# Turning one more quarter of the mixed activation with a transposing DMA in a two-layer encoder

## The chip, the cores and the metric

The kernel runs on one core of a Trainium2 chip. The metric is the device time of one execution in microseconds (us), as the median of several runs. The core has five engines with a queue of instructions each: TensorE (PE, matrix products and transposes), VectorE (DVE), ScalarE (ACT), GpSimd (POOL) and SyncE (SP), which here issues the DMA transfers. Each queue runs in order; engines wait for one another through semaphores. PEld is the weight load of TensorE, which overlaps its matmuls.

## The reference

The program is a trunk of two layers (DEPTH = 2) over 256 tokens of width 1024, all in float32. In each layer a normed input is projected; a branch A (gated linear attention) and a branch B (grouped-query attention) are formed; they are gated and mixed, and the mix goes through an output projection with a norm and a residual add:

```python
branch_a = (o_gla * jax.nn.silu(gg)) @ w_o_gla
branch_b = gqa_attention(q, k, v) @ w_o_attn
mixed = jax.nn.sigmoid(gate_a) * branch_a + jax.nn.sigmoid(gate_b) * branch_b
h = h + rms_norm(mixed @ w_out, g_mix_post)
gate, up = jnp.split(rms_norm(h, g_ffn_pre) @ w_ffn_in, 2, axis=-1)
h = h + rms_norm((jax.nn.silu(gate) * up) @ w_ffn_out, g_ffn_post)
```

A small embedding per layer follows. The case is about `mixed`, between the line that forms it and `mixed @ w_out`.

## The kernel before

**Tiling.** The 256 tokens are two halves of 128 (`hf` 0 and 1), each filling the partitions. Activations lie with tokens on the partitions; to be the stationary operand of a projection they must be turned, so that features lie on the partitions. Every float32 operand of a matmul is split into a high part (a cast on ScalarE, L112) and a low part (a subtraction on VectorE, L108), and a product is three matmuls: high by high, high by low, low by high (`mm3`, issued at L96). A `Split` object holds the turned and split activation: eight blocks of 128 features, in two groups of four.

**Weights** stream from HBM in units of 1 MB or less through two raw buffers (tag `raw`). ScalarE and VectorE split each unit in two pieces into `wh` and `wl`. When a projection is done with a unit, `ws.done()` starts the splitting of a further one, and with it the next load (L260 on SP, which waits until VectorE has freed the raw buffer).

**Two ways to turn.** `transpose_in` (L429) does four PE transposes of 128x128 into one PSUM bank (`aux`, L433), and then splits from PSUM with raised priority (`put`). `turn_words` (L391) goes without TensorE: a copy on ScalarE separates the two 16-bit halves of each word (L401), a DMA with transpose issued on SP turns them (L407), a second copy on ScalarE joins the halves again (L420), and then the same split follows, from SBUF. It takes three tiles of the pool `t512`, which has seven.

**Order.** Turning is a `Task`, a generator that is run up to its first `yield` when it is created; the number yielded says after how many ticks it goes on. A tick falls in `amode` after every six matmuls of 512 columns, or after twelve of 256. `turn_words` yields SENT = 3 between its first copy and the DMA, and LANDED = 9 between the DMA and the second copy; the PE way yields WAIT_MIX = 3. `Split.need` runs a task to its end where its result is about to be read. So ticks set where an instruction stands in the program. A compile-time scheduler then orders each engine's queue by priority and by what it holds ready, and can put an instruction well ahead of its place in the program (or, inside `high_priority(AHEAD)`, with a head start of 400); `issue_after` pins an order.

**Around the change.** The merge (L1203 to L1219) goes over two column halves `j` of 512, and in each over the two branches; each projection uses all four (`hf`, weight half) combinations. Branch A's product is multiplied by its gate into `sgate[0]`, branch B's into `sgate[1]`, and the two are added (L1212); the tile shows as `big_0gate` or `big_1gate`. That quarter of the mix, 128 tokens by 512 columns, is then handed to a turning task for the `Split` named `mixT` (shown as `big_0merge`, `big_1merge`). The output projection follows (`by_half`, L659, shown as `acc_0wout`): first the whole of `hf` 0, which reads group 0 of `mixT` and then group 1, as 48 matmuls of 512 columns; then `hf` 1, whose columns are cut into 512, 256 and 256, again with group 0 and then group 1. After each half, `after_out` does the norm with residual add and the norm ahead of the FFN: square sums on ScalarE (L471), the inverse root on GpSimd (L483, L487), products and adds on VectorE (L105, L531, L491), and then PE transposes of the normed half.

Of the kernel before, what the change touches and what calls it, by code (L numbers as in the profile page):

```python
# [50 lines left out]
def trunk_kernel(ctx: ExitStack, tc: tile.TileContext, a: dict, out: bass.AP):  # L51
# [52 lines left out]
    def vmul(out, in0, in1):  # L104
        nc.vector.tensor_tensor(out=out, in0=in0, in1=in1, op=ALU.mult)  # L105
# [323 lines left out]
    def transpose_in(sp, src, k, n, hf, plain=None):  # L429

        ps = aux()
        for i in range(n):
            nc.tensor.transpose(ps[:, i * P : (i + 1) * P], src[:, i * P : (i + 1) * P], ident)  # L433
        with tc.high_priority(AHEAD):
            sp.put(ps[:, : n * P], k, n, hf * P, P)
        if plain is not None:
            nc.scalar.copy(plain, ps[:, : n * P])
# [211 lines left out]
    def project(sp):  # L649

        o = [acc(), acc()]
        for kh in range(2):
            w = ws.take()
            for hf in range(2):
                amode(o[hf], sp, hf, kh * 4, w, kh == 0, kh == 1)
            ws.done()
        return o
# [146 lines left out]
    for l in range(DEPTH):  # L804
# [399 lines left out]
        mixT = Split()  # L1204
        ogate.need()
        for j in range(2):
            for br, src in enumerate((gT, aT)):
                for hf, o in enumerate(project(src)):
                    sl = [s[:, hf, j * 512 : (j + 1) * 512] for s in sgate]
                    vmul(sl[br], o, sl[br])  # L1210
                    if br == 1:
                        nc.vector.tensor_tensor(out=sl[0], in0=sl[0], in1=sl[1], op=ALU.add)  # L1212

                        def turn(src=sl[0], hf=hf):
                            yield WAIT_MIX
                            transpose_in(mixT, src, 4, 4, hf)

                        turn = turn() if j else mixT.turn_words(sl[0], 0, 4, hf)
                        mixT.makers[hf].append(Task(turn, part[0], j))  # L1219

        if l + 1 < DEPTH:
# [232 lines left out]
```

## Time and profile before

| | |
|---|---|
| median of 3 runs | 924.8 us |
| lowest and highest | 924.55 and 925.81 us |
| the profiled execution | 924.19 us |
| span in its profile | 922.5 us |
| clock of TensorE granted, mean | 0.997 |

The span runs from the first to the last instruction that the profiler recorded. In the rows shown below, a row of the timeline gives start, duration, engine, line, operation, what it writes and reads, how many instructions were merged into the row, and in brackets the idle time before it and what ended it. A row of the chain gives start, duration, engine, tile and line. Tile names carry the layer and the stage: `wl_0merge` is a low weight part of layer 0 allocated in the merge.

### The profile page before, as it was taken

How to read it: one execution, taken by the hardware profiler on the slowest of the kernel's cores; microseconds unless marked ns; L12 is line 12 of the kernel's file. 1: busy time of each engine (PE TensorE's matmuls, PEld its weight loads, DVE VectorE, ACT ScalarE, POOL GpSimd, SP SyncE). 2: the span in 40 equal slices, each digit the busy share in tenths (PEclk: the TensorE clock that was granted, in tenths of full speed). 3: DMA queues.
4: the chain of work that ended last, by engine and by line, in shares of the span. 5: the costliest groups of instructions: out<-in, count | busy, mean ns of one | idle time of the engine just before them, and what ended most of it. 6: DMA issues, size and time to landing. Idle time of an engine off the chain costs nothing.

```text
span 922.5 us, 12213 instructions
## 1 busy us (share of the span) xinstructions
PE 909.2 (99%) x4577; PEld 771.5 (84%) x4577; DVE 724.3 (79%) x921; ACT 626.1 (68%) x1002; POOL 82.6 (9%) x150
## 2 busy tenths in 40 slices
PE   8999999999999999999999999999999999999996
PEld 7999888888878888887889988888888788888885
DVE  4798977546579998998689789665666799989874
ACT  4668678746468787676765786776455788857663
POOL 3400211100000000000123002100001000000000
PEclk9999999999999999999999999999999999999998
DMA  7564456967377675847555524497564867666551
GB/s 233 171 213 152 137 167 161 291 201 227 95 239 239 174 249 199 267 146 241 176 183 183 183 92 143 143 241 250 194 199 136 276 206 221 217 248 174 184 181 47
DMA packets 119897, 177.12 MB, mean 192 GB/s; under 512 B 35159, under 2 KB 58199, under 8 KB 119838
## 3 DMA queue, kind: packets, MB, share of 16 engines
q1 hardware_dynamic: 119838, 176.34, 59.9%
q8 instruction: 36, 0.59, 0.3%
q14 instruction: 23, 0.19, 0.1%
HBM read 167.41 MB, written 1.05 MB: 183 GB/s over the span
## 4 chain that ended last, share of the span: by engine, by line
PE 75%; DVE 10%; DMA 6%; ACT 4%; issue 3%; POOL 2%; SPq 0%; POOLq 0%; ACTq 0%; DVEq 0%
PE acc_1ffnin L96 10%; PE acc_0ffnin L96 6%; PE acc_1gate L96 5%; PE acc_0gate L96 5%; PE acc_1merge L96 5%; PE acc_0merge L96 5%; PE acc_1ffnin L574 4%; DVE wl_0ffnin L108 3%; PE acc_1gqk L96 2%; PE acc_0rq L96 2%; PE acc_0gqk L96 2%; DMA raw_0ffnin<-in_w_ffn_out_dram 2%; PE acc_1ple L96 2%; PE acc_1gg L96 2%; PE acc_0gg L96 2%
## 5 line engine op out<-in xcount | busy, mean ns | idle before, releaser
L96 PE MATMUL acc_0ffnin<-wh_0ffnin,big_0ffnin 128*128 128x512 f32 x176 | 56.3, 392 | 0.0
L96 PE MATMUL acc_1ffnin<-wh_1ffnin,big_1ffnin 128*128 128x512 f32 x176 | 56.2, 391 | 0.0
L108 DVE TENSOR_TENSOR wl_1ffnin<-raw_1ffnin,wh_1ffnin 128x1024 fp32r<-128x1024 f32 x38 | 45.0, 1218 | 6.4 <-ACT wh_1ffnin L112 6.4
L112 ACT CAST wh_0ffnin<-raw_0ffnin 128x1024 fp32r<-128x1024 f32 x38 | 38.3, 1050 | 17.1 <-DMA raw_0ffnin<-in_w_ffn_out_dram 14.6
L112 ACT CAST wh_1ffnin<-raw_1ffnin 128x1024 fp32r<-128x1024 f32 x38 | 38.4, 1048 | 17.0 <-DMA raw_1ffnin<-in_w_ffn_out_dram 8.9
L108 DVE TENSOR_TENSOR wl_0ffnin<-raw_0ffnin,wh_0ffnin 128x1024 fp32r<-128x1024 f32 x38 | 44.9, 1219 | 6.1 <-ACT wh_0ffnin L112 6.1
L96 PEld LDWEIGHTS acc_1ffnin<-wh_1ffnin,big_1ffnin 128*128 128x128 f32 x176 | 33.0, 188 | 7.1 <-DVE big_1ffnin L108 0.2
L96 PEld LDWEIGHTS acc_0ffnin<-wh_0ffnin,big_0ffnin 128*128 128x128 f32 x176 | 33.0, 188 | 7.1 <-DVE big_0ffnin L108 0.2
L112 ACT CAST wh_0ffnin<-lent_0ffnin 128x1024 fp32r<-128x1024 f32 x30 | 30.2, 1050 | 10.2 <-DVE lent_0ffnin L289 4.0
L108 DVE TENSOR_TENSOR wl_0ffnin<-lent_0ffnin,wh_0ffnin 128x1024 fp32r<-128x1024 f32 x30 | 35.3, 1218 | 1.6 <-ACT wh_0ffnin L112 1.6
L112 ACT CAST wh_1ffnin<-lent_1ffnin 128x1024 fp32r<-128x1024 f32 x30 | 30.2, 1050 | 8.9 <-PE acc_1ffnin L96 3.5
L108 DVE TENSOR_TENSOR wl_1ffnin<-lent_1ffnin,wh_1ffnin 128x1024 fp32r<-128x1024 f32 x30 | 35.3, 1217 | 1.2 <-ACT wh_1ffnin L112 1.2
L96 PE MATMUL acc_0ffnin<-wl_0ffnin,big_0ffnin 128*128 128x512 f32 x88 | 34.4, 391 | 0.1
L96 PE MATMUL acc_1ffnin<-wl_1ffnin,big_1ffnin 128*128 128x512 f32 x88 | 34.4, 391 | 0.1
L574 PE MATMUL acc_1ffnin<-wh_1ffnin,mid_1ffnin 128*128 128x512 f32 x96 | 31.0, 390 | 0.0
L574 PE MATMUL acc_0ffnin<-wh_0ffnin,mid_0ffnin 128*128 128x512 f32 x96 | 31.0, 390 | 0.0
L96 PE MATMUL acc_1ffnin<-wh_1ffnin,big_1wout 128*128 128x512 f32 x96 | 30.4, 389 | 0.0
L96 PE MATMUL acc_0ffnin<-wh_0ffnin,big_0wout 128*128 128x512 f32 x96 | 30.3, 389 | 0.0
L108 DVE TENSOR_TENSOR wl_1gate<-raw_1gate,wh_1gate 128x1024 fp32r<-128x1024 f32 x14 | 16.5, 1221 | 15.2 <-ACT wh_1gate L112 15.2
L108 DVE TENSOR_TENSOR wl_0gate<-raw_0gate,wh_0gate 128x1024 fp32r<-128x1024 f32 x14 | 16.7, 1235 | 12.3 <-ACT wh_0gate L112 12.3
L96 PE MATMUL acc_0rq<-wh_start,big_start 128*128 128x384 f32 (+1 forms) x96 | 25.4, 349 | 0.9 <-ACT big_start L123 0.9
L96 PE MATMUL acc_1gate<-wh_1gate,big_0ple 128*128 128x512 f32 x80 | 24.8, 389 | 0.0
(659 smaller groups left out, 2964.4 us busy)
## 6 DMA issues: line engine op xcount, KB each, us to landing
raw_0ffnin<-in_w_ffn_out_dram SPq DMA_DIRECT2D x11, 1024.0 KB, 5.7
raw_1ffnin<-in_w_ffn_out_dram SPq DMA_DIRECT2D x11, 1024.0 KB, 5.0
lent_0ffnin<-in_w_ffn_in_dram SPq DMA_DIRECT2D x6, 1024.0 KB, 7.6
lent_1ffnin<-in_w_ffn_in_dram SPq DMA_DIRECT2D x6, 1024.0 KB, 5.3
raw_0rq<-in_w_in_dram SPq DMA_DIRECT2D x4, 1024.0 KB
raw_0v<-in_w_in_dram SPq DMA_DIRECT2D x4, 1024.0 KB
raw_0gg<-in_w_in_dram SPq DMA_DIRECT2D x4, 1024.0 KB, 5.1
raw_0gate<-in_w_o_gla_dram SPq DMA_DIRECT2D x4, 1024.0 KB, 5.9
```

What stands on the lines that cost most here:

```text
L96: return nc.tensor.matmul(o, lhsT, rhs, start=start, stop=stop)
L108: nc.vector.tensor_tensor(out=out, in0=in0, in1=in1, op=ALU.subtract)
L112: cast = nc.scalar.copy(hi, src)
L574: nc.tensor.matmul(o, x, y, start=first and k + n == 0, stop=k == 3 and n == 2, skip_group_check=not first)
```

## The change

The task for the second column half (`j` = 1) of the second token half (`hf` = 1) is made with `turn_words` instead of `transpose_in`. The second column half of the first token half keeps its PE transposes, and the first column half keeps `turn_words` for both token halves. Beside the way of turning, this changes the task's waits from WAIT_MIX (3 ticks, then everything) to SENT and LANDED (3 ticks to the DMA, 9 more to the copy back and the split). It is done in both layers.

```diff
@@ -1215,7 +1215,7 @@
                             yield WAIT_MIX
                             transpose_in(mixT, src, 4, 4, hf)
 
-                        turn = turn() if j else mixT.turn_words(sl[0], 0, 4, hf)
+                        turn = turn() if j and hf == 0 else mixT.turn_words(sl[0], 4 * j, 4, hf)
                         mixT.makers[hf].append(Task(turn, part[0], j))
 
         if l + 1 < DEPTH:
```

The core of `turn_words`, which the edited line now calls for this quarter too (here `hf` is given and `far` is false):

```python
def turn_words(self, src, k, n, hf=None, far=False):
...
    x = lambda: t512()[:, : n * P * (2 if hf is None else 1)]
    w = x()
    w16 = w.bitcast(U16)
    nc.scalar.copy(
        w16.rearrange("p (s c) -> p s c", s=2), src.bitcast(U16).rearrange("p (c s) -> p s c", s=2)
    )
    yield SENT
    r, z = [t[:, : n * P * (2 if hf is None else 1)] for t in halves(mid())] if far else (x(), None)
    r16 = r.bitcast(U16)
    nc.sync.dma_start_transpose(out=r16.rearrange("p (r t) -> p r t", t=P), in_=w16)
    yield LANDED
    z = x() if z is None else z
    z16 = z.bitcast(U16)
...
        else:
            nc.scalar.copy(z16.rearrange("p (c s) -> p s c", s=2), r16.rearrange("p (s c) -> p s c", s=2))
            self.put(z, k, n, hf * P, P)
```

## The prediction

> **What bounds the kernel now.** I read the page first: busy time and the chain that ended last. Then I read the chain in order of time around the two places where the edited task runs.
>
> ```profile
> span 922.5 us, 12213 instructions
> PE 909.2 (99%) x4577; PEld 771.5 (84%) x4577; DVE 724.3 (79%) x921; ACT 626.1 (68%) x1002; POOL 82.6 (9%) x150
> PE 75%; DVE 10%; DMA 6%; ACT 4%; issue 3%; POOL 2%; SPq 0%; POOLq 0%; ACTq 0%; DVEq 0%
> ```
>
> TensorE is busy 99% of the span and holds 75% of the chain, so what is taken off TensorE's own queue counts, unless another engine's answer is then late. ScalarE (68%) has room on average; whether it has room here is a question for its queue. The chain at the end of the merge, in layer 0 and then layer 1:
>
> ```profile
> 190.16 43.52 PE acc_0merge L96 x192
> 233.67 4.09 PE acc_0wout L96 x18
> 238.63 6.84 PE acc_0wout L96 x30
> 253.32 1.15 DVE wl_0wout L108
> 254.90 6.11 DMA raw_0wout<-in_w_ffn_in_dram
> ...
> 642.74 43.52 PE acc_1merge L96 x192
> 686.26 4.09 PE acc_1wout L96 x18
> 691.22 6.84 PE acc_1wout L96 x30
> 705.90 1.14 DVE wl_1wout L108
> 707.48 5.00 DMA raw_1wout<-in_w_ffn_in_dram
> ```
>
> The chain is TensorE through the merge and the first token half of the output projection. It breaks once between the 18th and the 19th matmul of that projection (237.76 to 238.63 in layer 0): there the eight PE transposes stand, after three ticks of six matmuls. After that it goes over VectorE's splitting of weights and a load of FFN weights. The two layers run alike, 452.6 us apart.
>
> **The change part by part.** The edit touches one task per layer: the turning of the second 512 columns for tokens 128 to 255. Removed are four PE transposes (one `transpose_in`). TensorE around them:
>
> ```profile
> 237.37 0.40 PE L96 MATMUL acc_0wout<-wh_0merge,big_0merge 128*128 128x512 f32 x1
> 237.60 1.03 PE L433 MATMUL aux_0merge<-ident,big_0gate 128*128 128x128 f32 x8
> 238.39 0.47 PE L96 MATMUL acc_0wout<-wh_0merge,big_0merge 128*128 128x512 f32 x1
> 238.70 0.39 PE L96 MATMUL acc_0wout<-wl_0merge,big_0merge 128*128 128x512 f32 x1
> ```
>
> The eight occupy the queue from 237.60 to 238.39, 0.79 us or 0.10 us each, since they are pipelined. Around them matmuls start 0.23 us apart (237.37 to 237.60), and one step after them is 0.31 us; I leave that bubble in place, because four transposes remain. So four transposes give 4 x 0.10 = **0.40 us** a layer, 0.79 us in two. All of it is on the chain. Bounds: nothing if what follows is late anyway, 0.87 us a layer if the whole gap were the second group's; I take 0.40.
>
> One rule of the Trainium skill would price this higher. "TensorE: Matmul & The Clock Gate", Part 4: PE-mode transpose, gives about 275 ns for one 128x128 transpose in a kernel, and eight at that price are an estimated 2.2 us. The trace agrees with such a duration (272 ns, row below) but not with such a step.
>
> The removed cast and subtraction out of PSUM come back from SBUF at nearly the same length. Added per layer are a copy into 16-bit planes (L401), a transposing DMA (L407) and a copy back (L420). The same three stand in the trace for the first 512 columns:
>
> ```profile
> 211.31 1.05 ACT L401 COPY t_0merge<-big_0gate 128x1024 uint16<-128x1024 uint16 x1 [2.80 <-DVE big_0gate L1212]
> 214.16 1.04 ACT L401 COPY t_0merge<-big_0gate 128x1024 uint16<-128x1024 uint16 x1
> 212.38 4.08 SPq L407 DMA_TRANSPOSE t_0merge<-t_0merge  x2
> 216.45 1.37 ACT L420 COPY t_0merge<-t_0merge 128x1024 uint16<-128x1024 uint16 x1 [1.25 <-DMA t_0merge<-t_0merge]
> 220.09 1.36 ACT L420 COPY t_0merge<-t_0merge 128x1024 uint16<-128x1024 uint16 x1
> 221.64 1.28 DVE L108 TENSOR_TENSOR big_0merge<-t_0merge,big_0merge 128x512 fp32r<-128x512 f32 x2
> L407 SPq DMA_TRANSPOSE t_0merge<-t_0merge x2: 1235/1244/1253, 212.4 to 215.2; - x2
> DMA to landing us min/median/max: 2.4/4.0/8.0
> ```
>
> That is 1.04 + 1.37 = 2.4 us more on ScalarE and 1.24 us more on SP's queue per layer. The first transfer lands 4.07 us after its issue (212.38 to 216.45); all transposing DMAs of the kernel lie between 2.4 and 8.0. From first copy to last subtraction the second half's path was 214.16 to 222.92, 8.8 us, with every wait in it. Now where these fall in the new place:
>
> ```profile
> 233.71 2.00 ACT L112 CAST wh_0merge<-raw_0merge 128x1024 fp32r<-128x1024 f32 x2 [3.43 <-PE acc_0merge L96]
> 238.23 1.07 ACT L112 CAST big_0merge<-aux_0merge 128x512 fp32r<-128x512 f32 x2 [2.52 <-PE aux_0merge L433]
> 242.84 0.60 ACT L471 ACTIVATE t_0wout<-acc_0wout 128x512 f32<-128x512 f32 x1 [3.53 <-PE acc_0wout L96]
> 245.56 0.60 ACT L471 ACTIVATE t_0wout<-acc_0wout 128x512 f32<-128x512 f32 x1 [2.03 <-PE acc_0wout L96]
> 234.44 0.69 DVE L1212 TENSOR_TENSOR big_0gate<-big_0gate,big_0gate 128x512 f32<-128x512 f32 x1
> 235.05 2.35 DVE L108 TENSOR_TENSOR wl_0merge<-raw_0merge,wh_0merge 128x1024 fp32r<-128x1024 f32 x2
> 231.75 6.60 SPq L260 DMA_DIRECT2D raw_0merge<-in_w_ffn_in_dram  x4
> 254.48 3.19 SPq L260 DMA_DIRECT2D raw_0wout<-in_w_ffn_in_dram  x4
> 251.12 0.40 PE L96 MATMUL acc_0wout<-wl_0merge,big_0merge 128*128 128x512 f32 x1
> ```
>
> The sum that is turned is ready at 235.13. ScalarE finishes its two weight casts at 235.71 and idles 2.52 us, so the first copy runs 235.71 to 236.75, covered by that idle time. If the cover were gone it would push the cast at 238.23, which TensorE needs for matmul 25 near 239.46. On SP the last two of the four loads wait until VectorE frees their buffer at 237.40, so the transposing DMA can go out at 236.75 and take 1.24 us; the loads behind it go 0.6 us later, and their weights are cast only from 248.75 on, so this costs nothing. No other issue follows before 254.48. Behind the loads instead, it would go out at 238.35.
>
> Landing: 236.75 + 4.07 = 240.8. The copy back ends near 242.2, the cast near 242.8, the subtraction near 243.5. ScalarE idles 3.53 us ahead of 242.84, VectorE is free until 243.56, so this is covered too. TensorE first reads the result just before 251.12 (one matmul after 250.9; 250.5 with 0.40 us saved): 7 us of slack by this sum, and 6 us by the older path's 8.8 us from 235.71.
>
> The wait added is the copy back's for the landing. Queued behind it on ScalarE, by time, are the two square sums at 242.84 and 245.56. Through GpSimd and VectorE they set when the normed first half is ready for its transposes:
>
> ```profile
> 251.90 1.42 DVE L491 SCALAR_TENSOR_TENSOR mid_0wout<-h,rstd_0wout,mid_0wout 128x512 f32<-128x512 f32 x2 [0.86 <-POOL rstd_0wout L487]
> 253.24 3.49 DVE L108 TENSOR_TENSOR wl_0wout<-raw_0merge,wh_0wout 128x1024 fp32r<-128x1024 f32 x3
> 253.65 1.03 PE L433 MATMUL aux_0wout<-ident,mid_0wout 128*128 128x128 f32 x8
> 248.75 1.03 ACT L112 CAST wh_0wout<-raw_0merge 128x1024 fp32r<-128x1024 f32 x1
> ```
>
> The normed half is complete at 253.32 and TensorE reaches it at 253.65, 0.33 us of slack. The whole row of square sum, scale, norm, weight split and next load hangs on the end of the first half's matmuls, and so moves 0.40 us earlier with them. That is why I let the gain reach the end. Nothing there is bound by a clock of its own: at most two raw buffers are under way, and each load starts on a release.
>
> **Sum:** 2 x 0.40 = 0.79 us of the profiled execution's 924.19 us (span 922.5 us), giving 923.4; that execution is 0.6 us under the median of 924.8, from which I get 924.8 - 0.8 = **924.0 us**. A measurement of this kernel can tell about 0.2%, 1.85 us, from no change, so this is a forecast of no visible change, with a slight lean down.
>
> **The rivals.**
>
> First, *slower: ScalarE's queue is held ahead of the first half's cast.* The compile-time scheduler orders ScalarE; if it puts the copy back in front of the cast at 238.23, the cast waits for landing and copy: 240.82 + 1.36 + 0.59 = 242.8, where TensorE wants it at 239.46. That is 3.3 us lost and 0.4 won, 2.9 a layer, 5.8 in all: **930.6 us**. For it: the copy back ran 11 us ahead of its twelve ticks in the first columns (12 x 6 x 0.23 = 16 us after the creation near 211.5, against 216.45), and ScalarE idled 1.25 us for the landing, so that order is not kept by ticks. Against it: the first half's cast has raised priority and its input is there at 238.2, 1.4 us after the transposing DMA's issue, below the 2.4 us minimum of the landings. It decides where the landing assumed by the scheduler is under 1.4 us. Chance 0.10.
>
> Second, *slower: the landing is late and holds the square sums.* If the transfer goes behind the loads or needs the 8.0 us maximum, it lands at 244.75; copy (1.36) and cast (0.54) end at 246.65, the first square sum with its read takes 0.68, the second starts at 247.33 instead of 245.16. Of these 2.2 us the slack takes 0.33, so 1.84 is lost and 0.4 won: +1.44 a layer, **927.7 us** at most. It decides from a landing near 242.9. For it: four weight loads surround the place. Against it: under the same loads the first columns took 4.07 us. Chance 0.14.
>
> The Trainium skill speaks against the change here: "VectorE: DVE Perf Modes", The three transpose paths, has 390 ns on TensorE against 1309 ns by DMA for 128x128 bf16, and its Rules for kernel authors take TensorE where PSUM will do. Exposed, four such differences would cost an estimated 3.7 us a layer; the trace shows the longer path too (8.8 us against 237.60 to 240.14), but under matmuls.
>
> Third, *faster: a transpose gives back its duration, not its step.*
>
> ```profile
> L433 PE MATMUL aux_0merge<-ident,big_0gate x8: 271/272/273, 237.6 to 238.4; 128*128 128x128 f32 x8
> ```
>
> 8 x 0.272 = 2.2 us: **922.6 us**. The starts (eight in 0.79 us) speak against it. Chance 0.06. This is where the 275 ns of the Trainium skill would lead.
>
> Fourth, *the gain is swallowed:* the load at 254.90 is the chain's, and its landing differs by 1.1 us between the layers (6.11 and 5.00), so a 0.4 us earlier issue may buy nothing: **924.8 us**. Against it: its release moves too. Chance 0.14.
>
> **How the numbers follow.** Forecast 0.56 (924.0, its own spread 923.3 to 925.2), then 0.10, 0.14, 0.06, 0.14. Slower by over 0.2%: the first rival and most of the second, with a little for orders that shift elsewhere in the kernel: 0.26. Faster: the third and a tail of the forecast, 0.10. Within: 0.64. The range runs from the third rival to the top of the second, 922.5 to 928.0, leaving out the first.
>
> **What would show it.** Right: four transposes instead of eight near 237.6, the next matmul near 238.0; the copies near 235.7 and 241 with no cast or square sum waiting behind; merge and projection 0.4 us shorter in both layers; the rest shifted as a block. Wrong: idle TensorE ahead of matmul 25 or ahead of the transposes near 253, or a lead gone again by 270. The prediction fails most likely through ScalarE's order around the copy back, which no row of before shows in this place.

## The result, and the profile after

The changed kernel takes 929.93 us (median of 5, 928.78 to 930.48) against 924.55 us before: a ratio of 1.0052, 95% interval 1.0039 to 1.0066. It is slower by about 4.8 us, where 0.8 us less was forecast. The profiled execution took 930.16 us (before: 924.19). Of two kernels in the table below, one execution each ran far longer at a low granted clock (1294.23 us for z made early, 1005.29 us for the transposes at 12 ticks); the ratios leave these two out.

The page's busy times of the kernel after, and its chain by engine:

```profile
span 928.4 us, 12207 instructions
PE 910.6 (98%) x4569; PEld 771.8 (83%) x4569; DVE 725.1 (78%) x921; ACT 629.5 (68%) x1006; POOL 82.8 (9%) x150
PE 67%; DVE 15%; DMA 6%; ACT 5%; issue 4%; POOL 2%; SPq 0%; POOLq 0%; ACTq 0%; DVEq 0%
```

ScalarE does 3.4 us more (4.8 were put for the two layers; in the stretches shown next it is 4.2), and TensorE has eight instructions fewer: the parts of the change are about as forecast. But the span grew by 5.9 us, and TensorE's share of the chain fell from 75% to 67%, to VectorE above all. So little work was added; something is waited for.

Where, shows a view by stretches. Each row runs from the first matmul of the output projection to the first matmul of the paired FFN blocks, the same work in every kernel. Columns: start and end, length, busy us of PE, PEld, DVE, ACT and POOL with their instructions, granted clock, DMA share, GB/s. Before, layers 0 and 1:

```profile
233.66:292.96 59.30, 58.70 (x289) 48.31 (x288) 42.07 (x53) 38.38 (x66) 4.16 (x9) 1.00 0.65 202
686.24:744.80 58.56, 58.28 (x289) 48.38 (x288) 42.03 (x53) 38.62 (x66) 4.58 (x9) 1.00 0.67 204
```

After, layers 0 and 1:

```profile
233.59:296.03 62.44, 60.07 (x285) 49.22 (x284) 43.13 (x54) 40.55 (x68) 4.88 (x9) 0.97 0.65 195
688.65:750.02 61.37, 58.66 (x286) 48.06 (x285) 43.08 (x54) 40.67 (x68) 5.65 (x9) 1.00 0.68 199
```

The stretch is longer by 3.14 us and 2.81 us, together 5.95 us, which is the difference of the spans. (Between the stretches the kernel after is 0.66 us quicker and behind the second 0.68 us slower, so the rest cancels.) Inside it, the timeline of TensorE after, layer 0 (the first three rows lie around the removed transposes, the others where the turned quarter is first read):

```profile
237.30 0.40 PE L96 MATMUL acc_0wout<-wh_0merge,big_0merge 128*128 128x512 f32 x1
237.53 0.60 PE L433 MATMUL aux_0merge<-ident,big_0gate 128*128 128x128 f32 x4
237.88 0.48 PE L96 MATMUL acc_0wout<-wh_0merge,big_0merge 128*128 128x512 f32 x1
...
250.27 0.28 PE L96 MATMUL acc_0wout<-wh_0merge,big_0merge 128*128 128x256 f32 x1
252.07 1.32 PE L433 MATMUL aux_0wout<-ident,mid_0wout 128*128 128x128 f32 x8 [1.52 <-DVE mid_0wout L491]
253.40 0.49 PE L96 MATMUL acc_0ffnin<-wh_0wout,big_0wout 128*128 128x512 f32 x1
253.86 0.50 PE L96 MATMUL acc_0ffnin<-wl_0wout,big_0wout 128*128 128x512 f32 x1
254.58 0.80 PE L96 MATMUL acc_0wout<-wh_0merge,big_0merge 128*128 128x512 f32 x1 [0.21 <-ACT big_0merge L112]
```

The saving is there: four transposes, and the next matmul comes 0.35 us after their start instead of 0.79 us. Then TensorE reaches the second weight half of the second token half at 250.4, in time. But its queue doesn't hold those matmuls next. The transposes of the normed first half stand there, which before stood behind twelve of those matmuls, and TensorE waits 1.52 us for VectorE to finish the norm. The matmuls on the turned quarter follow at 254.58, mixed with first FFN matmuls.

The reason stands on ScalarE. Its timeline after, layer 0:

```profile
235.55 1.04 ACT L401 COPY t_0merge<-big_0gate 128x1024 uint16<-128x1024 uint16 x1
238.16 0.58 ACT L112 CAST big_0merge<-aux_0merge 128x512 fp32r<-128x512 f32 x1 [1.58 <-PE aux_0merge L433]
242.28 0.60 ACT L471 ACTIVATE t_0wout<-acc_0wout 128x512 f32<-128x512 f32 x1 [3.53 <-PE acc_0wout L96]
...
247.62 0.64 ACT L471 ACTIVATE t_0wout<-h 128x512 f32<-128x512 f32 x1 [1.87 <-DVE h L531]
...
248.25 1.35 ACT L420 COPY t_0merge<-t_0merge 128x1024 uint16<-128x1024 uint16 x1
249.46 0.62 ACT L471 ACTIVATE t_0wout<-h 128x512 f32<-128x512 f32 x1
...
250.08 1.98 ACT L112 CAST wh_0wout<-raw_0merge 128x1024 fp32r<-128x1024 f32 x2
252.76 1.25 ACT L112 CAST big_0wout<-aux_0wout 128x512 fp32r<-128x512 f32 x2 [0.71 <-PE aux_0wout L433]
253.90 0.62 ACT L112 CAST big_0merge<-t_0merge 128x512 fp32r<-128x512 f32 x1
```

The first copy runs at 235.55, as forecast (235.71). The copy back, forecast for 240.8, runs at 248.25. ScalarE idles 3.53 us ahead of 242.28, long enough, and the copy back waited for no transfer when its turn came (its row has no idle time). The transfer itself went out at 236.62 and landed 3.1 us later. So it was not the transfer that was late; the copy back stands late in ScalarE's queue, right behind the first square sum over `h`. Its cast then stands behind two weight casts and the casts of the normed half, 5.65 us after it. Layer 1 has the same order and the same 1.52 us of waiting:

```profile
702.68 0.64 ACT L471 ACTIVATE t_1wout<-h 128x512 f32<-128x512 f32 x1 [1.87 <-DVE h L531]
...
703.31 1.35 ACT L420 COPY t_1merge<-t_1merge 128x1024 uint16<-128x1024 uint16 x1
```

Four theories could explain such a place, and the experiments tell them apart. **A**: a buffer. The copy back writes a tile `z` of the pool `t512`, and the scratch tiles of the square sums come from that pool too; if buffers of a pool are handed out in the program order of their first write, `z`, which stands after 12 ticks, is behind the two scratch tiles of the norm, which stands after 8. **B**: the added transfer and copies cost the time wherever they stand. **C**: the late place in the program and the lack of raised priority. **The price rival**: a transpose was worth another amount.

A plain shortage of buffers would be another theory. The number of buffers was not varied, but layer 1 speaks against it: there the pool's tiles of the first columns are last read at 677.7, and from the first copy (690.62) to the copy back (703.31) at most five of its tiles are in use, the edited task's three and the two scratch tiles, for seven buffers. The copy back is as late there as in layer 0.

### The profile page after: what moved, and what is told of

Its sections match the earlier page's. It is cut to its first block, busy times and chain, and to the rows that moved or that the text cites. A ratio compares the mean times of both kernels' runs of the same rounds, so it can differ in the third digit from the quotient of the medians.

```text
span 928.4 us, 12207 instructions
## 1 busy us (share of the span) xinstructions
PE 910.6 (98%) x4569; PEld 771.8 (83%) x4569; DVE 725.1 (78%) x921; ACT 629.5 (68%) x1006; POOL 82.8 (9%) x150
## 3 DMA queue, kind: packets, MB, share of 16 engines
HBM read 167.41 MB, written 1.05 MB: 181 GB/s over the span
## 4 chain that ended last, share of the span: by engine, by line
PE 67%; DVE 15%; DMA 6%; ACT 5%; issue 4%; POOL 2%; SPq 0%; POOLq 0%; ACTq 0%; DVEq 0%
PE acc_1ffnin L96 6%; PE acc_0ffnin L96 6%; PE acc_0gate L96 5%; PE acc_1gate L96 5%; PE acc_1merge L96 5%; PE acc_0merge L96 5%; DVE wl_1ffnin L108 4%; DVE wl_0ffnin L108 3%; PE acc_1gqk L96 2%; PE acc_0rq L96 2%; PE acc_0gqk L96 2%; PE acc_1ple L96 2%; PE acc_0gg L96 2%; PE acc_1gg L96 2%; PE acc_0v L96 2%
## 5 line engine op out<-in xcount | busy, mean ns | idle before, releaser
L96 PE MATMUL acc_0gate<-wh_0gate,big_start 128*128 128x512 f32 x80 | 24.8, 389 | 0.0
```

Source lines behind the costliest of these rows:

```text
L96: return nc.tensor.matmul(o, lhsT, rhs, start=start, stop=stop)
```

## The experiments

The ratio is to the kernel before on the same chip, with its 95% interval. The edits show only the lines that matter; the flags in them (`early`, `soon`, `half`) are set for the edited task alone.

| kernel | median us | ratio | interval |
|---|---|---|---|
| after | 929.93 | 1.0052 | 1.0039 to 1.0066 |
| z first written early | 922.53 | 0.9985 | 0.9973 to 0.9998 |
| 5 ticks to the copy back | 922.78 | 0.9984 | 0.9973 to 0.9995 |
| raised priority | 927.66 | 1.0030 | 1.0016 to 1.0044 |
| z made early, not written | 929.82 | 1.0053 | 1.0034 to 1.0072 |
| z from another pool | 923.04 | 0.9990 | 0.9979 to 1.0001 |
| before, transposes fivefold | 929.66 | 1.0064 | 1.0050 to 1.0077 |
| before, transposes at 12 ticks | 925.80 | 1.0016 | 1.0007 to 1.0025 |
| change in layer 0 alone | 926.10 | 1.0023 | 1.0012 to 1.0034 |
| 6 ticks to the copy back | 927.78 | 1.0039 | 1.0026 to 1.0052 |
| scratch from another pool | 922.39 | 0.9975 | 0.9964 to 0.9986 |

**z first written early.** Right behind the DMA:

```diff
+            if early:
+                z = x()
+                nc.gpsimd.memset(z[:, 0:1], 0.0)
             yield LANDED
```

> Kernel after, but the result buffer of the copy back (z, pool t512) is made right behind the transposing DMA and its first column is zeroed there by GpSimd (one 128x1 memset a layer); copy back and split keep their place in the program (12 ticks). Theory A: the buffers of a pool are handed out in the program order of their first write, and in after z stood behind the two scratch buffers of the square sums of the first token half, so the copy back could not be ordered ahead of the first square sum over h. With z written early it can. Expected by A: copy back near 241, nothing waiting, TensorE's order as before, about 0.8 us less than before: 923.5 to 924.5 us, 5 to 6 us under after. Theory B (the added transfer and the 2.4 us of ScalarE work a layer cost the time wherever they stand): 929 to 931 us. Theory C (the late place in the program, 12 ticks, and the lack of raised priority cost it): unchanged, 929 to 931 us.

By the ratios it lies 0.67% or 6.2 us under the kernel after, with one instruction more per layer. ScalarE in layer 0 (lines are shifted by 3 in this kernel):

```profile
233.65 1.05 ACT L401 COPY t_0merge<-big_0gate 128x1024 uint16<-128x1024 uint16 x1
236.27 0.59 ACT L112 CAST big_0merge<-aux_0merge 128x512 fp32r<-128x512 f32 x1 [1.57 <-PE aux_0merge L436]
237.91 1.35 ACT L423 COPY t_0merge<-t_0merge 128x1024 uint16<-128x1024 uint16 x1 [1.05 <-DMA t_0merge<-t_0merge]
239.29 0.62 ACT L112 CAST big_0merge<-t_0merge 128x512 fp32r<-128x512 f32 x1
240.38 0.60 ACT L474 ACTIVATE t_0wout<-acc_0wout 128x512 f32<-128x512 f32 x1 [0.47 <-PE acc_0wout L96]
```

This is the picture of the prediction. The copy back waits 1.05 us for its landing (237.91, 3.2 us after the first copy's end at 234.70), the cast follows, and the square sum still waits 0.47 us for TensorE, so nothing was held up. The stretch of the projection, layers 0 and 1:

```profile
231.69:289.88 58.19, 57.91 (x286) 47.93 (x284) 42.14 (x53) 40.91 (x68) 4.60 (x9) 1.00 0.68 210
682.80:740.98 58.18, 57.90 (x286) 47.93 (x284) 42.20 (x53) 40.96 (x68) 4.38 (x9) 1.00 0.69 211
```

Against before it is 1.11 us and 0.38 us shorter. B falls: transfer and copies are all there. C falls too, since place and priority of the copy back are those of the kernel after.

**z made early, not written.** The same without the memset line.

> Kernel after, with z made right behind the transposing DMA but not written there: the same as the run with the early first write, without that write. A, in the form that the first write decides and not the line that makes the tile: as after, 929 to 931 us. If the line that makes the tile decides: 923.5 to 924.5 us.

It is as slow as the kernel after. What counts is the first write to the tile, not the line that makes it.

**Raised priority.**

```diff
-            with tc.issue_after(ws.cast.ins) if far else nullcontext():
+            with tc.issue_after(ws.cast.ins) if far else tc.high_priority(AHEAD) if soon else nullcontext():
```

> Kernel after, with the raised priority (a head start of 400) that the PE way has, on copy back, cast and subtraction of the edited task; place and buffer as in after. A: the copy back stays behind the first square sum over h, since the buffer order does not change; only the cast and the subtraction move up. Part of the loss goes: 925 to 928 us. C: 923.5 to 924.5 us. B: 929 to 931 us.

As A expects, a part comes back, though its interval and that of the kernel after just overlap. C, which expected all of it back, lies outside the interval. ScalarE in layer 0:

```profile
246.76 0.63 ACT L471 ACTIVATE t_0wout<-h 128x512 f32<-128x512 f32 x1 [1.88 <-DVE h L531]
...
247.39 1.36 ACT L420 COPY t_0merge<-t_0merge 128x1024 uint16<-128x1024 uint16 x1
248.61 0.62 ACT L471 ACTIVATE t_0wout<-h 128x512 f32<-128x512 f32 x1
...
249.23 0.60 ACT L112 CAST big_0merge<-t_0merge 128x512 fp32r<-128x512 f32 x1
```

The copy back has not moved from its place behind the first square sum over `h`, whatever its priority; only the cast moved up.

**5 and 6 ticks to the copy back.** LANDED is replaced by 5, or by 6, for the edited task alone; with SENT = 3 that makes 8 and 9 ticks, and the norm of the first half is written down at the eighth.

> Kernel after, but the edited task waits 5 instead of 9 ticks between the DMA and the copy back, 8 in all, so that copy, split and z stand in the program just ahead of the norm of the first token half. A: z is then ahead of the scratch buffers, time as for the early first write, 923.5 to 924.5 us. C: faster as well, by the place; alone this run does not tell A from C. B: 929 to 931 us.

> Kernel after with 6 instead of 9 ticks between DMA and copy back: 9 ticks in all, one more than the kernel with 5. The eighth tick is the last of the first token half, and behind it the norm of that half is written down. A: z is now behind the scratch of the square sums, the copy back goes behind the first square sum over h again, and the whole step from fast to slow lies between 5 and 6; cast and subtraction stand earlier than in after, so the loss is like that with raised priority: 926 to 929 us. C (a late place costs gradually): 922.5 to 924 us, near the kernel with 5.

By the ratios, one tick makes 5 us. With 5 the copy back stands ahead of the square sums and the time is under that of before; with 6 it stands behind the first square sum over `h` once more. A place that costs by degrees would not step like that. ScalarE with 5, then with 6:

```profile
240.31 1.35 ACT L420 COPY t_0merge<-t_0merge 128x1024 uint16<-128x1024 uint16 x1 [0.99 <-DMA t_0merge<-t_0merge]
...
242.83 0.60 ACT L471 ACTIVATE t_0wout<-acc_0wout 128x512 f32<-128x512 f32 x1 [0.52 <-PE acc_0wout L96]
```

```profile
245.75 0.64 ACT L471 ACTIVATE t_0wout<-h 128x512 f32<-128x512 f32 x1 [1.87 <-DVE h L531]
...
246.39 1.35 ACT L420 COPY t_0merge<-t_0merge 128x1024 uint16<-128x1024 uint16 x1
```

**Another pool, from both sides.** First `z` leaves `t512`: the transfer's target and `z` become the halves of one tile of the pool `mid`. That tile is first written by the DMA, so this run changes the pool and the first write together.

```diff
-            r, z = [t[:, : n * P * (2 if hf is None else 1)] for t in halves(mid())] if far else (x(), None)
+            r, z = [t[:, : n * P * (2 if hf is None else 1)] for t in halves(mid())] if far or half else (x(), None)
```

> Kernel after, but the two buffers behind the transposing DMA (its target and the copy back's result z) are the halves of one tile of another pool (mid), written from the DMA on; place in the program as in after (12 ticks), no instruction more. A (buffer order of the pool t512 against the scratch of the square sums): z is free of that order, time as with the early first write, 922 to 924 us. C (late place, low priority): 929 to 931 us.

Then `z` stays, and the scratch of the first half's square sums behind the projection leaves `t512` (`other[0]` is true only there):

```diff
-        ss, r, junk = small(3, "ss"), small(1, "rstd"), mid() if parts[0].shape[-1] > 512 else t512()
+        ss, r, junk = small(3, "ss"), small(1, "rstd"), mid() if parts[0].shape[-1] > 512 or other[0] else t512()
```

> Kernel after with its 9 ticks and with z as it was; only the scratch of the square sums of the first token half after the output projection comes from the pool mid instead of t512. A: nothing of t512 stands ahead of z any more, time as with the early first write, 922 to 924 us. C and B: 929 to 931 us.

Both are fast. The second is the strongest run of the set: task, place, priority and buffer of the copy back are untouched, two unrelated scratch tiles are taken from elsewhere, and 0.77% or 7.1 us go. ScalarE in layer 0 of that kernel has the copy back ahead of the square sums again:

```profile
238.45 0.59 ACT L112 CAST big_0merge<-aux_0merge 128x512 fp32r<-128x512 f32 x1 [1.57 <-PE aux_0merge L433]
240.03 1.35 ACT L420 COPY t_0merge<-t_0merge 128x1024 uint16<-128x1024 uint16 x1 [0.99 <-DMA t_0merge<-t_0merge]
241.41 0.62 ACT L112 CAST big_0merge<-t_0merge 128x512 fp32r<-128x512 f32 x1
242.56 0.60 ACT L471 ACTIVATE mid_0wout<-acc_0wout 128x512 f32<-128x512 f32 x1 [0.53 <-PE acc_0wout L96]
```

**The price of a transpose.** The kernel before, with each of the four transposes done five times:

```diff
+            for _ in range(times_):
                 nc.tensor.transpose(ps[:, i * P : (i + 1) * P], src[:, i * P : (i + 1) * P], ident)
...
-                            transpose_in(mixT, src, 4, 4, hf)
+                            transpose_in(mixT, src, 4, 4, hf, times_=5 if hf else 1)
```

> Kernel before, in which each of the four PE transposes of the second token half in the edited task is done five times over into the same place: 16 transposes more per layer, 32 in all. The price by their step in the trace of before (0.10 us) is 1.6 us a layer, 3.2 us in all, 927 to 928 us; by their duration (0.272 us) 4.4 us a layer, 8.7 us in all, 932 to 934 us.

The time, 5.9 us more, lies between the two answers, and the trace says why:

```profile
237.04 2.78 PE L434 MATMUL aux_0merge<-ident,big_0gate 128*128 128x128 f32 x24
239.58 0.47 PE L96 MATMUL acc_0wout<-wh_0merge,big_0merge 128*128 128x512 f32 x1
```

24 transposes take 2.54 us of the queue, 0.106 us each, so 16 more take 1.7 us a layer, 3.4 us in all. The stretches of this kernel are 1.81 and 2.17 us longer than before, near that price and far from 4.4 us a layer. The rest, some 2.5 us by the ratio, is not in the transposes. Part of it shows as waits for split weights in the FFN (1.2 us and 0.4 us in this profile's waits of TensorE, below), which the list of the kernel before does not have; why a later start meets more of them was not tried.

```profile
PE acc_1ffnin L96 <- DVE wl_1ffnin L108: 1.2, 2, 0.8
PE acc_0ffnin L96 <- DVE wl_0ffnin L108: 0.4, 1, 0.4
```

**Lateness without the DMA.** In the kernel before, `yield 12 if hf else WAIT_MIX` in place of `yield WAIT_MIX`.

> Kernel before, with PE transposes, but the second token half's task waits 12 ticks instead of 3, the place that it has in after. A: a turned quarter that is ready only where it is read costs time by any way of turning: cast and subtraction out of PSUM stand late, TensorE idles or is reordered there; 926 to 931 us. B (the DMA and the extra copies cost the time): no transfer here, 924 to 925 us.

It costs 0.16%, about 1.5 us: the direction of A, less than A's figures, and clear of B. TensorE again waits for the norm of the first half, 1.2 us a layer:

```profile
PE aux_0wout L433 <- DVE mid_0wout L491: 1.2, 1, 1.2
```

A quarter that is turned where it is read costs by either way, but the DMA way, whose cast was 5.65 us behind its copy, costs three times as much.

**One layer.** The condition becomes `j and (hf == 0 or l == 1)`.

> The change in layer 0 alone; layer 1 as in before. The profiles put 2.5 us of the loss between the merges of layer 0 and layer 1 and 3.5 us behind the merge of layer 1. If the parts add: 926 to 927.5 us. If the loss comes from one layer alone or is made up later: 924 to 925 us, or 929 and more.

0.23%, about 2.1 us, a little under half of the whole, as if the parts add; layer 1 alone was not run. The stretch of layer 0 is as long as in the kernel after, that of layer 1 as before:

```profile
232.94:295.20 62.26, 60.11 (x285) 49.18 (x284) 43.13 (x54) 40.64 (x68) 5.32 (x9) 0.97 0.63 197
687.81:746.40 58.59, 58.31 (x290) 48.38 (x288) 42.22 (x53) 38.27 (x66) 4.58 (x9) 1.00 0.65 204
```

## Why the prediction was wrong, by its steps

- **The bound** held. What is lost is lost on TensorE's queue, between the projection and the paired FFN blocks.
- **The price of four transposes, 0.40 us a layer**, held on the queue (0.44 us in the kernel after: 0.79 less 0.35). In the four repaired kernels the stretch is 0.38 to 0.44 us shorter than before in layer 1. In layer 0 it is 0.66 to 1.17 us shorter, more than the transposes explain. In the kernel with the early first write it is 1.11 us: TensorE's busy time fell by 0.79 us and its idle time from 0.60 us (59.30 less 58.70) to 0.28 us (58.19 less 57.91). The four repaired kernels stand at ratios of 0.9975 to 0.9990; the forecast of 0.8 us would be 0.9991, inside three of the four intervals.
- **The added work** (2.4 us on ScalarE, 1.24 us on SP) and its cover held: in the repaired kernels it lies in idle time and nothing waits behind it. From issue to copy back it took 3.2 us (234.73 to 237.91) where 4.07 us was put.
- **The step that failed is "Landing: 236.75 + 4.07 = 240.8. The copy back ends near 242.2".** It took for granted that an instruction goes into its engine's queue when its input is there and the engine is free, because the first columns had done so. Inputs and engine were free, but the turn of the tile to write to had not come: in all these runs the pool `t512` behaves as if it hands its buffers out in the program order of first writes. For the first columns no scratch tile of that pool stood between; here two did. That the task takes three tiles of a pool of seven was known; in which order they are given, the prediction does not ask.
- **The size** follows from there. The copy back came 7.5 us late (248.25 for 240.8), its cast 11.7 us late (253.90 for 242.2), and TensorE's queue was put in another order around it. In each layer TensorE waits 2.1 us for norms (below, the waits of TensorE after, 250 to 275): 1.5 us for that of the first half, which now stands first, and 0.6 us at 272 for that of the second; for the cast itself it waits 0.2 us. In layer 1 this is nearly all: idle time in the stretch grew by 2.43 us, busy time by 0.38 us. In layer 0 idle time grew by 1.77 us and busy time by 1.37 us. Most of that busy time goes with the lower granted clock (0.97) in this execution: the kernel with z made early and not written has the same order at a clock of 1.00, and its layer 0 is busy 58.73 us, not 60.07, and about 1.0 us shorter (last row below). The small rest was not taken apart.

```profile
PE aux_0wout L433 <- DVE mid_0wout L491: 2.1, 2, 1.5
PE acc_0wout L96 <- ACT big_0merge L112: 0.2, 1, 0.2
```

```profile
230.97:292.44 61.47, 58.73 (x286) 48.07 (x284) 43.12 (x54) 40.68 (x68) 5.14 (x9) 1.00 0.64 199
```

- **The rivals.** The first, with 930.6 us, came near in time by luck, and not in mechanism: it had the copy back too early in ScalarE's queue, holding the others; it was too late and held by them. The second (a late landing) and the fourth (a gain swallowed by the weight load) did not happen. The load in layer 0 landed 4.97 to 5.88 us after its issue in the repaired kernels, where it took 6.11 us before, and so gave more back, not less; whether the change did that or scatter is open. The third is refuted by the 0.106 us step, although its 922.6 us lies among the repaired kernels' medians (922.39 to 923.04): they got there with four transposes at 0.4 us a layer and less waiting and slow matmuls in layer 0. What would make the prediction wrong was named rightly, ScalarE's order around the copy back. A chance of 0.26 for slower was too low for an order that no row showed.

## What to carry to other kernels

Where a scheduler places work by itself, a moved instruction brings its output buffer along: look which other tiles of the same pool are first written between its old and its new place in the program, and who their writers wait for. An instruction that starts late although its engine idles and its inputs have landed is to be suspected of waiting for its tile's turn; here the instruction right ahead of it in the queue, a square sum that has nothing to do with it, named the tile. In this kernel the fault was cheap to mend, by an early first write, a nearer place or another pool, and then the change gained 0.10% to 0.25% where 0.09% was forecast.

## What was not expected of the hardware

In two profiles the granted clock over layer 0's stretch was 0.97 (the kernel after, and the change in layer 0 alone), with first matmuls on the turned quarter of 0.80 us behind a wait of 1.52 us or 1.54 us for the norm. In layer 1 of the kernel after, behind a wait of the same length, it was 1.00 and the first matmul took 0.50 us:

```profile
709.64 0.50 PE L96 MATMUL acc_1wout<-wh_1merge,big_1merge 128*128 128x512 f32 x1 [0.22 <-ACT big_1merge L112]
```

The kernel with z made early and not written has the same order and a wait of 1.54 us in layer 0, and there too the clock was 1.00 and that matmul took 0.50 us. So the wait and the order do not decide it by themselves; what does was not tried.
